# State update of a pair moved behind its prompt-state product, py in a projection bank, scaled x double buffered

## The chip, the cores and the metric

The kernel runs on one core of one Trainium2 chip. The metric is device time in microseconds (us) for one execution of the whole program. Before the change it is 2816.27 us, the median of three runs (2815.08 to 2816.45).

The engines are named as the profile names them: PE (TensorE, matmuls; PEld are its weight loads), DVE (VectorE), ACT (ScalarE), POOL (GpSimd) and SP (SyncE, which here only issues DMAs). PE writes into PSUM, which has eight banks of 128 x 512 fp32; DVE and ACT read them. "L718" is line 718 of the kernel before.

## The reference, cut to what matters

One layer for 384 tokens (256 prompt tokens, and 8 running streams of 16 tokens). The change lies in the state space branch. For each of 8 groups, with 8 heads of 64 channels and a state of 128:

```
cum = cumsum(dt * A)
y   = ((C B^T) * decay) @ (x * dt)            # within the chunk
y  += (C @ h) * exp(cum)                      # from the state that came in
h   = h * exp(last) + B^T @ (x * dt * w_end)  # the new state, an output
y  += d_skip * x;  y *= silu(z);  grouped RMSNorm
```

Before it stands the combined projection `u @ w_in` (pool, z, x/B/C, dt, gates), after it the gate products, the output projection and a squared-ReLU MLP.

## The kernel before, in words

All large products are made in three passes of 128-wide matmuls: weights and activations are split into a high and a low fp32r part, and `mm3` (L76, L77, L78) issues high x high, high x low, low x high. The weights come in tiles of 512 KB. For each tile SP issues the load (L61), ACT makes the high part `wh` (L68), DVE makes the low part `wl` by a subtraction (L69). `w`, `wh` and `wl` have three buffers each. One projection (`proj`) is two such tiles, 2 x 8 x 3 = 48 matmuls of 128 x 384 into one PSUM bank. It needs `wl` for its third matmul.

The state space stage (L496 to L856) goes through 8 groups. A group has six projections with a causal convolution behind them (B as `BT`, C as `CT`, four of x) and four of z. Behind each of them DVE reads the bank (L516 for `cbuf`, L829 for z) and the rest is DVE and ACT work on SBUF. A group's four x tiles are two pairs; a pair is `S`, its fields are:

- `hs`, the running streams' states of the pair (1 MB, loaded by `pload`, decayed by `dside` L703, updated by `state`, stored to `new_ssm_s` by a DMA that POOL issues, L731). Two buffers: a load waits until the store of the pair before last has landed.
- `trs`, the pair's x transposed, in two PSUM banks (`t_trx`); `xside` (L651) scales it twice, into `xdt` and `xdw` (four DVE operations, L656), scales `yi` into `yis` (L663), and sends the scaled x of the running streams through DRAM into another layout, `xst` (L670 to L679).
- `E`, the decay matrix times C B^T (`eside`): twelve DVE operations (L689), ACT exponentials, two DVE products (L700).
- `Y`, two banks: `t_yT` and `t_Y`. `pp`, the new prompt state: `t_pp`. `yi`, C times the incoming state: `t_yi`. `yi` of one pair and `pp` of the pair before share one bank, `py`.
- `su`, the update of the running streams' states: `state` (L710) makes four banks with eight matmuls of half height (64 rows, L718), and four DVE additions into `hs` (L727).

PSUM is two pools: two banks `mm` (`mmtile`), which projections take in turn, and six banks `ss` (`sstile`) for the rest, `py` among them.

PE's order is written out: `lump` puts a set of matmuls behind the last one issued. In a group there are two blocks of fp32 matmuls between the projections. The **first block** stands behind the fifth projection (third x): `t_cb`, `t_trB`, `t_trx` of pair 0, `t_yT` and `t_Y` of the pair before (pair 1 of the group before), `t_yi`, `t_pp`. The **second block** stands behind the tenth projection (fourth z): `t_trx` of pair 1, `t_yT`, `t_Y` of pair 0, `t_yi`, `t_pp`. `state` stands elsewhere: that of pair 0 behind the third z projection, that of pair 1 behind the CT projection of the next group. The last pair's is put into the first gate product (`gate_b(0)`, after five of its eight weight tiles), and its `Y` and `pp` follow behind that product.

On DVE, ACT, POOL and SP a scheduler sets the order when the program is built, by priority (program order) and by when it thinks operands will be there. On the chip each of these queues works in that fixed order.

`xdt` and `xdw` have one buffer each before the change, so `xside` of a pair cannot write them until `t_Y` and `t_pp` of the pair before have read them.

`gate_b` writes its three sigmoid blocks into a pool of its own, `gbp` (L484), three buffers of 128 x 512.

Of the kernel before, what the change touches and what calls it, by code (L numbers as in the profile page):

```python
# [6 lines left out]
F32 = mybir.dt.float32  # L7
# [7 lines left out]
P = 128  # L15
T = 384
TP = 256
NB = 8
# [15 lines left out]
def build(ctx, tc, io):  # L34
# [98 lines left out]
    def three(name):  # L133
        return [sstile(f"{name}_{b}") for b in range(3)]
# [346 lines left out]
            if nb == 0:  # L481
                dt_turn(srcs)

    gbp = main.enter_context(tc.tile_pool(name="gbp", bufs=3, side="right"))  # L484

    def gate_b(nb, hook=None):
        o = three(f"pj_gb{nb}")

        def done(b):
            t = gbp.tile([P, 512], F32, tag="gbt", name=f"gbt{nb}_{b}")  # L490
            s.activation(t, o[b], AF.Sigmoid, scale=yx[:, b : b + 1])
            gp.dma_start(gb_scr[nb][:, b], t)

        moving(o, [(io["w_gb"][nb, kp], f"gb{nb}_{kp}") for kp in range(8)], xg, 0, done, hook=hook)

    with tc.tile_pool(name="phd", bufs=2, reuse_waits="tile") as pd, tc.tile_pool(  # L496
# [34 lines left out]
        def lump(fn):  # L531
            with behind(last[0]):
                last[0] = fn()
# [115 lines left out]
            v.tensor_tensor(D.cbm, D.cb, cst[:, C_MASK : C_MASK + 512], ALU.mult)  # L649

        def xside(S):  # L651
            S.xdt = pd.tile([P, 2, 3, P], F32, tag="xdt", name=f"xdt{S.nm}", bufs=1)
            S.xdw = pd.tile([P, 2, 3, P], F32, tag="xdw", name=f"xdw{S.nm}", bufs=1)
            for q, tv in enumerate(S.trs):
                for o, i in ((S.xdt, 3), (S.xdw, 6)):
                    v.tensor_tensor(  # L656
                        o[:, q].rearrange("p b (h q) -> p b h q", h=2),
                        tv,
                        tok[:, i : i + 3, S.h0 + q * 2 : S.h0 + q * 2 + 2].unsqueeze(3).to_broadcast([P, 3, 2, 64]),
                        ALU.mult,  # L660
                    )
            S.yis = pd.tile([P, 2, P], F32, tag="yis", name=f"yis{S.nm}", bufs=1)
            v.tensor_tensor(  # L663
                S.yis.rearrange("p j (h q) -> p (j h) q", h=2),
                S.yi.rearrange("p (h q) -> p h q", h=4),
                tok[:, 10, S.h0 : S.h0 + 4].unsqueeze(2).to_broadcast([P, 4, 64]),
                ALU.mult,
            )
            xhl = pd.tile([P, 2, 2, P], F32R, tag="xhl", name=f"xhl{S.nm}", bufs=1)
            s.activation(xhl[:, 0], S.xdw[:, :, 2, :], AF.Copy)  # L670
            v.tensor_tensor(xhl[:, 1], S.xdw[:, :, 2, :], xhl[:, 0].bitcast(F32), ALU.subtract)
            xscr = x_scr[S.qd]
            sy.dma_start(xscr, xhl.bitcast(F32))
            S.xst = pd.tile([P, 4, 2 * P], F32R, tag="xst", name=f"xst{S.nm}", bufs=1)
            for p4 in range(4):
                for h2 in range(2):
                    sy.dma_start(
                        S.xst[h2 * 64 + p4 * 16 : h2 * 64 + p4 * 16 + 16].bitcast(F32),
                        xscr.rearrange("(q h r) l j n -> h l r q (j n)", q=4, h=2)[h2, p4 % 2],  # L679
                    )  # L680
# [26 lines left out]
                ALU.mult,  # L707
            )

        def state(S, tiles=(sstile, sstile)):  # L710
            def t_su():
                hs = S.hs.rearrange("p (r h) n -> p h r n", h=2)
                for r2, tile_ in zip((0, 2), tiles):
                    su = [tile_(f"su{S.nm}_{r2}_{h}") for h in range(2)]
                    for r in range(2):
                        for h in range(2):
                            t = slice(h * 64, h * 64 + 64)
                            i = te.matmul(  # L718
                                su[h][:, r * 256 : r * 256 + 256],
                                S.D.bs[t, r2 + r, :],  # L720
                                S.xst[t, r2 + r, :],
                                start=True,
                                stop=True,
                            )
                    for h in range(2):
                        hr = hs[:, h, r2 : r2 + 2]
                        v.tensor_tensor(hr, hr, su[h].rearrange("p (r n) -> p r n", r=2), ALU.add)  # L727
                return i

            lump(t_su)  # L730
            gp.dma_start(io["new_ssm_s"][S.qd], S.hs)  # L731
# [46 lines left out]
        for g in range(G + 1):  # L778
            if g == G:
                dside(prev.p[1])  # L780
                gate_b(0, {4: lambda: state(prev.p[1], (mmtile, sstile))})
                py = mmtile("pp_last")
                lump(lambda: t_yT(prev.p[1]))
                lump(lambda: t_Y(prev.p[1]))
                lump(lambda: t_pp(prev.p[1], py))
                final(prev.p[1])
                gate_b(1)
                finish(prev)
                break
            u0 = 17 + g * 10  # L790
            D = Pair()
            D.g = g
            D.p = [pair(D, jp) for jp in range(2)]
            D.xs, D.zs = [], []
            D.BT = conv(u0, 32 + g, "BT", 2)
            pload(D.p[0])
            if g:
                dside(prev.p[1])
            D.CT = conv(u0 + 1, 40 + g, "CT", 2)
            if g:  # L800
                state(prev.p[1])
            D.xs.append(conv(u0 + 2, g * 4, "xs", 6))
            cload(D.p[0])
            cside(D)
            D.xs.append(conv(u0 + 3, g * 4 + 1, "xs", 6))
            D.xs.append(conv(u0 + 4, g * 4 + 2, "xs", 6))
            S = D.p[0]
            lump(lambda: t_cb(D))
            mside(D)
            lump(lambda: t_trB(D))  # L810
            bside(D)
            lump(lambda: t_trx(S))
            if g:
                lump(lambda: t_yT(prev.p[1]))
                lump(lambda: t_Y(prev.p[1]))
            S.py = sstile(f"py{S.nm}")
            lump(lambda: t_yi(S))
            if g:
                lump(lambda: t_pp(prev.p[1], S.py))
            if g:  # L820
                final(prev.p[1])
            xside(S)
            D.xs.append(conv(u0 + 5, g * 4 + 3, "xs", 6))
            eside(S, 0)

            def zproj(j):
                ps = proj(in_units(u0 + 6 + j), xg, f"z{g}_{j}")
                z = pd.tile([P, T], F32, tag="zs", name=f"zs{g}_{j}", bufs=7)
                v.tensor_tensor(z, ps, rstd, ALU.mult)  # L829
                s.activation(z, z, AF.Silu)  # L830
                D.zs.append(z)

            zproj(0)
            if g:
                finish(prev)
            pload(D.p[1])
            eside(S, 1)
            zproj(1)
            dside(S)
            zproj(2)  # L840
            state(S)
            cload(D.p[1])
            zproj(3)
            S1 = D.p[1]
            lump(lambda: t_trx(S1))
            lump(lambda: t_yT(S))
            lump(lambda: t_Y(S))
            S1.py = sstile(f"py{S1.nm}")
            lump(lambda: t_yi(S1))
            lump(lambda: t_pp(S, S1.py))  # L850
            final(S)
            xside(S1)
            eside(S1, 0)
            eside(S1, 1)
            prev = D
# [20 lines left out]
    with ExitStack() as phe:  # L876
        pe1 = phe.enter_context(tc.tile_pool(name="phe", bufs=1, reuse_waits="tile"))
        pe2 = phe.enter_context(tc.tile_pool(name="phe2", bufs=3, reuse_waits="tile"))
        ab = []

        def aload():
# [7 lines left out]
                ab.append((h, l))  # L889

        for nb in (2, 3):
            gate_b(nb, {kp: aload for kp in range(8)})
        chain[0] = False
        main.close()
        mp = mpool.enter_context(tc.tile_pool(name="mp", bufs=1, side="right", reuse_waits="tile"))
        pe3 = phe.enter_context(tc.tile_pool(name="phe3", bufs=1, reuse_waits="tile"))
        for nb in range(4):
            ma = mp.tile([P, 3, 512], F32, tag="mar", name=f"mar{nb}", bufs=1)
            gb = pe3.tile([P, 3, 512], F32, tag="gbr", name=f"gbr{nb}")
            sy.dma_start(ma, ma_scr[nb])  # L900
            sy.dma_start(gb, gb_scr[nb])
            o = three(f"pj_sp{nb}")

            def done(b):
                v.tensor_tensor(gb[:, b], o[b], gb[:, b], ALU.mult)
                v.tensor_tensor(ma[:, b], ma[:, b], gb[:, b], ALU.add)

            moving(o, [(io["w_ssd"][nb, kp], f"sp{nb}_{kp}") for kp in range(16)], ab, 0, done, hook={3: merge} if nb else None)
            mtok[0] = ma
# [397 lines left out]
```

## Time and profile before

| | |
|---|---|
| median of 3 runs | 2816.27 us |
| profiled execution | 2816.05 us |
| its span, first to last instruction | 2814.3 us |
| PE busy | 2800.4 us |
| DVE busy | 1544.6 us |
| ACT busy | 1085.1 us |
| POOL busy | 88.2 us |
| PE clock granted | 0.998 |
| DMA moved | 451.39 MB |

A row of the timeline gives the start of an instruction from the start of the span, its duration, engine, line, operation, and in brackets the idle time before it and what ended it. Matmuls are pipelined, so a row's duration is longer than its step: the step is the difference of two starts. DVE operations also overlap by about 0.09 us, so for these too the step is the difference of two starts.

### The profile page before, as it was taken

Reading aid. Unit: us, or ns where it says so; the run is one execution under the profiler, and the core shown is the slowest. Engines: PE = TensorE matmul, PEld = TensorE weight load, DVE = VectorE, ACT = ScalarE, POOL = GpSimd, SP = SyncE. Lnnn points to the kernel's source line nnn. Section 1 sums busy time; section 2 is a strip of 40 time slices with the busy share of each in tenths; the row PEclk is TensorE's granted clock in tenths of the full one; section 3 lists DMA queues with packets and bytes.
Section 4 is the critical chain, followed back from the end, with each engine's and each line's share of the span. In section 5 each row is a group of like instructions: output and inputs, shape, how many; then the busy total and the mean of one; then the engine's idle time right before and its main releaser. Section 6 shows DMA issues by size and latency. Waiting matters only on the chain.

```text
span 2814.3 us, 39013 instructions
## 1 busy us (share of the span) xinstructions
PE 2800.4 (100%) x15663; PEld 2546.4 (90%) x15663; DVE 1544.6 (55%) x2219; ACT 1085.1 (39%) x1586; POOL 88.2 (3%) x143
## 2 busy tenths in 40 slices
PE   9999999999999999999999999999999999999998
PEld 8998889999999999988888888989899998989897
DVE  6575335788787878856333335434444444444446
ACT  5443224445454545434322235433233332323233
POOL 0000000010010001010000000000000000000000
PEclk9999999999999999999999999999999999999999
DMA  7434445555656566557544543433333333443433
GB/s 269 132 124 148 139 142 200 193 202 188 217 192 206 199 214 200 194 178 233 176 144 162 180 143 109 142 130 127 128 127 128 128 128 127 128 128 128 130 127 125
DMA packets 140933, 451.39 MB, mean 160 GB/s; under 512 B 17808, under 2 KB 39632, under 8 KB 135760
## 3 DMA queue, kind: packets, MB, share of 16 engines
q1 hardware_dynamic: 132624, 412.97, 44.7%
q0 software_dynamic: 8128, 35.93, 3.5%
q8 instruction: 123, 2.02, 0.3%
q14 instruction: 58, 0.48, 0.1%
HBM read 407.11 MB, written 41.72 MB: 159 GB/s over the span
## 4 chain that ended last, share of the span: by engine, by line
PE 98%; DMA 1%; DVE 0%; ACT 0%; SPq 0%; issue 0%; DVEq 0%; ACTq 0%
PE pj_up L77 6%; PE pj_up L78 6%; PE pj_up L76 6%; PE wd L108 6%; PE wd L109 6%; PE wd L107 6%; PE pj_x L76 5%; PE pj_x L78 5%; PE pj_x L77 5%; PE pj_z L76 3%; PE pj_z L78 3%; PE pj_z L77 3%; PE pj_sp L107 3%; PE pj_sp L108 3%; PE pj_sp L109 3%; PE pj_gb L107 2%
## 5 line engine op out<-in xcount | busy, mean ns | idle before, releaser
L78 PE MATMUL pj_up<-x1h,wl_up 128*128 128x384 f32 x1024 | 343.0, 335 | 0.7 <-DVE wl_up L69 0.7
L76 PE MATMUL pj_up<-x1h,wh_up 128*128 128x384 f32 x1024 | 343.2, 335 | 0.5 <-ACT x1h L1033 0.5
L77 PE MATMUL pj_up<-x1l,wh_up 128*128 128x384 f32 x1024 | 343.0, 335 | 0.6 <-DVE x1l L1038 0.6
L69 DVE TENSOR_TENSOR wl_wd<-w_wd,wh_wd 128x1024 fp32r<-128x1024 f32 x127 | 155.7, 1226 | 261.9 <-ACT wh_wd L68 261.9
L108 PE MATMUL wd<-wl_wd,hh 128*128 128x512 f32 x762 | 296.7, 389 | 0.0
L109 PE MATMUL wd<-wh_wd,hl 128*128 128x512 f32 x762 | 296.6, 389 | 0.0
L107 PE MATMUL wd<-wh_wd,hh 128*128 128x512 f32 x762 | 296.3, 389 | 0.0
L68 ACT ACTIVATE wh_wd<-w_wd 128x1024 fp32r<-128x1024 f32 x127 | 134.8, 1061 | 350.6 <-PE wd L109 284.0
L69 DVE TENSOR_TENSOR wl_up<-w_up,wh_up 128x1024 fp32r<-128x1024 f32 x128 | 156.9, 1226 | 197.7 <-ACT wh_up L68 197.5
L68 ACT ACTIVATE wh_up<-w_up 128x1024 fp32r<-128x1024 f32 x128 | 135.9, 1062 | 323.0 <-PE pj_up L77 259.8
L76 PE MATMUL pj_x<-xgh,wh_x 128*128 128x384 f32 x768 | 258.9, 337 | 0.0
L78 PE MATMUL pj_x<-xgh,wl_x 128*128 128x384 f32 x768 | 256.6, 334 | 0.0
L77 PE MATMUL pj_x<-xgl,wh_x 128*128 128x384 f32 x768 | 256.6, 334 | 0.0
L77 PEld LDWEIGHTS pj_up<-x1l,wh_up 128*128 128x128 f32 x1024 | 192.6, 188 | 1.4 <-DVE x1l L1038 1.2
L76 PEld LDWEIGHTS pj_up<-x1h,wh_up 128*128 128x128 f32 x1024 | 192.8, 188 | 1.3 <-ACT x1h L1033 1.0
L78 PEld LDWEIGHTS pj_up<-x1h,wl_up 128*128 128x128 f32 x1024 | 192.7, 188 | 1.0 <-DVE wl_up L69 1.0
L76 PE MATMUL pj_z<-xgh,wh_z 128*128 128x384 f32 x512 | 171.9, 336 | 0.0
L78 PE MATMUL pj_z<-xgh,wl_z 128*128 128x384 f32 x512 | 171.1, 334 | 0.0
L77 PE MATMUL pj_z<-xgl,wh_z 128*128 128x384 f32 x512 | 171.0, 334 | 0.0
L108 PEld LDWEIGHTS wd<-wl_wd,hh 128*128 128x128 f32 x762 | 143.0, 188 | 29.8 <-DVE wl_wd L69 0.4
L109 PEld LDWEIGHTS wd<-wh_wd,hl 128*128 128x128 f32 x762 | 143.0, 188 | 29.7
L107 PEld LDWEIGHTS wd<-wh_wd,hh 128*128 128x128 f32 x762 | 143.0, 188 | 29.6
(318 smaller groups left out, 5727.0 us busy)
## 6 DMA issues: line engine op xcount, KB each, us to landing
w_up<-w_up SPq DMA_DIRECT2D x128, 512.0 KB, 3.4
w_wd<-w_down SPq DMA_DIRECT2D x128, 512.0 KB, 3.4
w_x<-w_in SPq DMA_DIRECT2D x96, 512.0 KB, 4.8
w_z<-w_in SPq DMA_DIRECT2D x64, 512.0 KB, 3.9
w_sp<-w_ssd SPq DMA_DIRECT2D x64, 512.0 KB, 3.4
w_ga<-w_ga SPq DMA_DIRECT2D x32, 512.0 KB, 3.5
w_pp<-w_pp SPq DMA_DIRECT2D x32, 512.0 KB, 3.4
hs<-ssm SPq DMA_DIRECT2D x16, 1024.0 KB, 6.0
```

The costliest lines, as they stand in the source:

```text
L68: s.activation(h, w, AF.Copy)
L69: v.tensor_tensor(l, w, h.bitcast(F32), ALU.subtract)
L76: te.matmul(out, wh, xh, start=first, stop=False)
L77: te.matmul(out, wh, xl, start=False, stop=False)
L78: return te.matmul(out, wl, xh, start=False, stop=last)
L107: te.matmul(o[b], mh, wh[:, c], start=k == 0, stop=False)
L108: te.matmul(o[b], mh, wl[:, c], start=False, stop=False)
L109: last[0] = te.matmul(o[b], ml, wh[:, c], start=False, stop=k == nk - 1)
```

## The change

Five edits, all in the state space stage and around it:

- `state` is issued behind `t_pp`, inside the next fp32 block: pair 0's at the end of the second block, pair 1's at the end of the next group's first block, the last pair's at the end of the block between the two gate products. All its tiles come from `ss`.
- `py` comes from the `mm` pool.
- `xdt` and `xdw` take two buffers (6 KB more per partition).
- `xside` is called ahead of `state` and `final`, so that its scaling comes ahead of the sums with `Y` on DVE.
- `gate_b` takes its three blocks as one tile in a buffer of the `hs` kind (and, for the last two products, in a pool `pe4` that the later reads `gbr` share); the pool `gbp` goes.

```diff
-    gbp = main.enter_context(tc.tile_pool(name="gbp", bufs=3, side="right"))
-    def gate_b(nb, hook=None):
+    def gate_b(nb, pool, tag, hook=None):
         o = three(f"pj_gb{nb}")
+        n = NB * 256 if tag == "hs" else 1536
+        t = pool.tile([P, n], F32, tag=tag, name=f"gbt{nb}")[:, :1536].rearrange("p (b n) -> p b n", b=3)
         def done(b):
-            t = gbp.tile([P, 512], F32, tag="gbt", name=f"gbt{nb}_{b}")
-            s.activation(t, o[b], AF.Sigmoid, scale=yx[:, b : b + 1])
-            gp.dma_start(gb_scr[nb][:, b], t)
+            s.activation(t[:, b], o[b], AF.Sigmoid, scale=yx[:, b : b + 1])
+            gp.dma_start(gb_scr[nb][:, b], t[:, b])
...
-            S.xdt = pd.tile([P, 2, 3, P], F32, tag="xdt", name=f"xdt{S.nm}", bufs=1)
-            S.xdw = pd.tile([P, 2, 3, P], F32, tag="xdw", name=f"xdw{S.nm}", bufs=1)
+            S.xdt = pd.tile([P, 2, 3, P], F32, tag="xdt", name=f"xdt{S.nm}")
+            S.xdw = pd.tile([P, 2, 3, P], F32, tag="xdw", name=f"xdw{S.nm}")
...
             if g == G:
                 dside(prev.p[1])
-                gate_b(0, {4: lambda: state(prev.p[1], (mmtile, sstile))})
+                gate_b(0, pd, "hs")
                 py = mmtile("pp_last")
                 lump(lambda: t_yT(prev.p[1]))
                 lump(lambda: t_Y(prev.p[1]))
                 lump(lambda: t_pp(prev.p[1], py))
+                state(prev.p[1])
                 final(prev.p[1])
-                gate_b(1)
+                gate_b(1, pd, "hs")
...
             D.CT = conv(u0 + 1, 40 + g, "CT", 2)
-            if g:
-                state(prev.p[1])
...
-            S.py = sstile(f"py{S.nm}")
+            S.py = mmtile(f"py{S.nm}")
             lump(lambda: t_yi(S))
             if g:
                 lump(lambda: t_pp(prev.p[1], S.py))
+            xside(S)
             if g:
+                state(prev.p[1])
                 final(prev.p[1])
-            xside(S)
...
             zproj(2)
-            state(S)
             cload(D.p[1])
             zproj(3)
...
-            S1.py = sstile(f"py{S1.nm}")
+            S1.py = mmtile(f"py{S1.nm}")
             lump(lambda: t_yi(S1))
             lump(lambda: t_pp(S, S1.py))
+            xside(S1)
+            state(S)
             final(S)
-            xside(S1)
```

The scheduler's answer to it, as the two built programs show: PE's order changes only by the place of `su`. On DVE, behind the second block, one subtraction moves: the `wl` of the first half of the next group's CT projection stands ahead of the `Y` sums before, and behind the `cbuf` read of the BT projection after.

More of the change, by code (lines that the diff above doesn't have):

```diff
@@ L708, in dside, with state @@
             )
-        def state(S, tiles=(sstile, sstile)):
+        def state(S):
             def t_su():
                 hs = S.hs.rearrange("p (r h) n -> p h r n", h=2)
-                for r2, tile_ in zip((0, 2), tiles):
-                    su = [tile_(f"su{S.nm}_{r2}_{h}") for h in range(2)]
+                for r2 in (0, 2):
+                    su = [sstile(f"su{S.nm}_{r2}_{h}") for h in range(2)]
                     for r in range(2):
@@ L878, in build @@
         pe2 = phe.enter_context(tc.tile_pool(name="phe2", bufs=3, reuse_waits="tile"))
+        pe4 = phe.enter_context(tc.tile_pool(name="phe4", bufs=1, reuse_waits="tile"))
         ab = []
@@ L891, in build @@
         for nb in (2, 3):
-            gate_b(nb, {kp: aload for kp in range(8)})
+            gate_b(nb, pe4, "gbt", {kp: aload for kp in range(8)})
         chain[0] = False
@@ L895, in build @@
         mp = mpool.enter_context(tc.tile_pool(name="mp", bufs=1, side="right", reuse_waits="tile"))
-        pe3 = phe.enter_context(tc.tile_pool(name="phe3", bufs=1, reuse_waits="tile"))
         for nb in range(4):
             ma = mp.tile([P, 3, 512], F32, tag="mar", name=f"mar{nb}", bufs=1)
-            gb = pe3.tile([P, 3, 512], F32, tag="gbr", name=f"gbr{nb}")
+            gb = pe4.tile([P, 1536], F32, tag="gbt", name=f"gbr{nb}").rearrange("p (b n) -> p b n", b=3)
             sy.dma_start(ma, ma_scr[nb])
```

## The prediction, made before the changed kernel ran

> **What bounds the kernel now.** I read the page first, then PE's waits, then the timelines of PE and DVE around the two fp32 blocks of one group.
>
> ```profile
> span 2814.3 us, 39013 instructions
> ...
> PE 2800.4 (100%) x15663; PEld 2546.4 (90%) x15663; DVE 1544.6 (55%) x2219; ACT 1085.1 (39%) x1586; POOL 88.2 (3%) x143
> ...
> PE 98%; DMA 1%; DVE 0%; ACT 0%; SPq 0%; issue 0%; DVEq 0%; ACTq 0%
> ```
>
> The chain that ended last is PE for 98% of the span. So a step of PE removed is time won, and each wait of PE added is time lost. PE's waits for others (total, times, longest) hold little, for `wl` only this:
>
> ```profile
> PE pj_up L78 <- DVE wl_up L69: 0.7, 1, 0.7
> ```
>
> It is not in the state space stage, where PE does not wait at all. What the change can win there is steps between matmuls; what it can lose is new waits. The standing `su` in PE's timeline:
>
> ```profile
> 903.66 0.34 PE L78 MATMUL pj_z<-xgh,wl_z 128*128 128x384 f32 x1
> 903.93 0.75 PE L718 MATMUL su<-xst,bst 64*128 64x256 f32 x8
> 904.61 0.44 PE L76 MATMUL pj_z<-xgh,wh_z 128*128 128x384 f32 x1
> 904.88 0.34 PE L77 MATMUL pj_z<-xgl,wh_z 128*128 128x384 f32 x1
> ```
>
> and the exit of the second block into BT, the next group's first projection, with the start of CT, its second:
>
> ```profile
> 917.65 0.44 PE L76 MATMUL pj_x<-xgh,wh_x 128*128 128x384 f32 x1
> ...
> 926.08 0.33 PE L76 MATMUL pj_x<-xgh,wh_x 128*128 128x384 f32 x1
> 926.26 0.33 PE L77 MATMUL pj_x<-xgl,wh_x 128*128 128x384 f32 x1
> ```
>
> A step from one projection matmul to the next is 0.17 to 0.18 us (926.08 to 926.26); BT takes 917.65 to 926.08, 8.43 us.
>
> **What the change removes.** A projection step into `su` is 0.27 (903.66 to 903.93) and out of it 0.27 (904.61 to 904.88), each 0.10 over 0.17. `su` itself is 0.68 (903.93 to 904.61) and stays. In the block, the exit takes the place of the exit that `pp` had; the entry becomes `pp` to `su`, which no trace shows. Bounds: both extras go (0.20 per update, 3.2 us for 16) or the new entry costs twice the old (0, nothing won). I take one extra saved, 0.10 x 16 = **-1.6 us**, since the nearest row, the entry from a projection, costs 0.10. The Trainium skill (TensorEngine Tiling (Array Packing), Key Properties) says that a change of tiling mode drains the engine. `pp` (128*32) to `su` (64*128) is such a change, so by that page the entry is not free either; the rows above agree, with 0.10 us a switch.
>
> **What the change moves on DVE: the CT wait.** The trace shows DVE's instructions in the order of the program. These are its rows around the standing `su` and the second block:
>
> ```profile
> 904.51 2.47 DVE L727 TENSOR_TENSOR hs<-hs,su 128x512 f32<-128x512 f32 x4
> 906.90 1.22 DVE L69 TENSOR_TENSOR wl_x<-w_x,wh_x 128x1024 fp32r<-128x1024 f32 x1
> ...
> 913.24 0.56 DVE L829 TENSOR_TENSOR zs<-pj_z,rstd 128x384 f32<-128x384 f32 x1 [1.97 <-PE pj_z L78]
> 914.20 1.22 DVE L69 TENSOR_TENSOR wl_x<-w_x,wh_x 128x1024 fp32r<-128x1024 f32 x1 [0.40 <-ACT wh_x L68]
> 915.34 0.61 DVE L743 SCALAR_TENSOR_TENSOR xs<-xs,vec,Y 128x384 f32<-128x384 f32 x1
> ```
>
> ```profile
> 926.87 0.55 DVE L516 TENSOR_TENSOR cbuf<-pj_x,rstd 128x384 f32<-128x384 f32 x1
> 927.33 1.22 DVE L69 TENSOR_TENSOR wl_x<-w_x,wh_x 128x1024 fp32r<-128x1024 f32 x1
> ```
>
> The `wl_x` at 914.20 is the low part for CT's first half. In the changed program's order it stands behind the `cbuf` read of BT, in the place of the row at 927.33, in each of the seven groups that have a next one. CT's third matmul needs it. Between 915.34 and 926.87 DVE does not idle, so I move sums: the queue up to `cbuf` loses that `wl_x` (914.20 to 915.34, 1.14) and its wait (0.40), and gains the four additions of `su` (904.51 to 906.90, 2.39), which now come in this stretch. `cbuf` starts at 926.87 - 1.54 + 2.39 = 927.72, `wl_x` 0.46 later (926.87 to 927.33) at 928.18 and ends 1.22 on, at 929.40; a weight load puts the matmul 0.19 later, at 929.6:
>
> ```profile
> L78 PEld LDWEIGHTS pj_up<-x1h,wl_up 128*128 128x128 f32 x1024 | 192.7, 188 | 1.0 <-DVE wl_up L69 1.0
> ```
>
> PE, with `su` in the block, starts CT at 926.08 + 0.68 = 926.76 and its third matmul at 927.1. It waits 2.5 us. Even with no backlog on DVE, `cbuf` cannot be read before BT ends: about 0.2 + 0.46 + 1.22 + 0.19 - 0.35 = 1.7. I take 2.4, near the upper end because the backlog is made of rows. 7 x 2.4 = **+16.8 us**. Behind the waiting matmul stands all of PE's queue, so nothing makes it good.
>
> The last second block has the first gate product behind it, and there `wl` of the third weight tile falls behind the same backlog:
>
> ```profile
> 1205.53 0.50 PE L107 MATMUL pj_gb<-wh_gb,xgh 128*128 128x512 f32 x1
> 1205.87 0.40 PE L108 MATMUL pj_gb<-wl_gb,xgh 128*128 128x512 f32 x1
> ```
>
> ```profile
> 1214.74 2.35 DVE L69 TENSOR_TENSOR wl_gb<-w_gb,wh_gb 128x1024 fp32r<-128x1024 f32 x2
> ...
> 1226.69 2.48 DVE L727 TENSOR_TENSOR hs<-hs,su 128x512 f32<-128x512 f32 x4 [6.22 <-PE su L718]
> ```
>
> A weight tile lasts about 4.1 us there (five from 1205.53 to `su`, just ahead of 1226.69). The third tile's `wl` starts at 1214.74 - 1.54 + 2.39 = 1215.6 and serves a matmul at 1217.0; PE wants it at 1205.53 + 0.68 + 8.2 + 0.34 = 1214.8. **+2.2 us**, once.
>
> **The bank wait in the first block.** The built program gives the third and fourth `su` tile of the first block the banks of the two `trx` tiles. Their readers are the four scaled-x operations, so `su` now waits for DVE:
>
> ```profile
> 870.10 0.44 PE L76 MATMUL pj_x<-xgh,wh_x 128*128 128x384 f32 x1
> ```
>
> ```profile
> 868.25 0.61 DVE L524 SCALAR_TENSOR_TENSOR cacc<-cbuf,vec,cacc 128x384 f32<-128x384 f32 x1
> 868.77 0.61 DVE L743 SCALAR_TENSOR_TENSOR xs<-xs,vec,Y 128x384 f32<-128x384 f32 x1
> ...
> 872.22 0.55 DVE L656 TENSOR_TENSOR xdt<-trx,tok 128x384 f32<-128x384 f32 x1
> 872.68 0.55 DVE L656 TENSOR_TENSOR xdw<-trx,tok 128x384 f32<-128x384 f32 x1
> ```
>
> With two buffers the four operations come before the `Y` sums: from 868.77 on four steps of 0.47 (872.22 to 872.68) with one convolution step (0.52) among them. The last starts at 868.77 + 3 x 0.47 + 0.52 = 870.70 and ends at 871.25; with the weight load, 871.45. PE would reach the fourth tile at 870.10 + 0.34 = 870.45 to 870.5. It waits 0.95 us, in seven first blocks: **+6.7 us**. Were the scaled x where it was (872.68), it would be 3 us. In the second block the same banks are free in time: DVE's read of z starts at 913.24, four steps of 0.47 behind it end by 915.7, and `su` comes at 917.65.
>
> **The z wait.** The four additions also fall into the stretch between the first block and the third z projection:
>
> ```profile
> 894.99 0.56 DVE L141 SCALAR_TENSOR_TENSOR ny_g<-na_g,ny_g 128x384 f32<-128x384 f32 x1
> 895.58 2.21 DVE L764 SCALAR_TENSOR_TENSOR zs<-zs,vec,ny_g 128x384 f32<-128x384 f32 x4
> 897.71 0.55 DVE L829 TENSOR_TENSOR zs<-pj_z,rstd 128x384 f32<-128x384 f32 x1
> 898.17 1.22 DVE L69 TENSOR_TENSOR wl_z<-w_z,wh_z 128x1024 fp32r<-128x1024 f32 x1
> ```
>
> This `wl_z` serves the third z projection's second half, whose third matmul stands at
>
> ```profile
> 900.02 0.33 PE L78 MATMUL pj_z<-xgh,wl_z 128*128 128x384 f32 x1
> ```
>
> In the new order the z read stands ahead of the last Newton step (0.59) and the four products (2.13). It starts at 894.99 + 2.39 = 897.4; plus 0.46 + 0.59 + 2.13 + 1.22 + 0.19 the matmul could start at 902.0. PE is there at 900.02 + 0.68 + 0.95 = 901.65. Bounds 0 and 0.8 a group, 0.35 taken: 7 x 0.35 = **+2.5 us**.
>
> **What costs nothing, and its cover.** `py` in a projection bank: the projection two later waits for its readers `yis` and the copy of `pp`, a whole projection (8.4 us) away. `gate_b` in an `hs` buffer: the store of that buffer was issued a product earlier. The moved store and the load behind it:
>
> ```profile
> 907.28 0.54 POOL L731 DMA_DIRECT2D new_ssm_s<-hs  x1 [8.62 <-DVE hs L727]
> ```
>
> ```profile
> 912.33 0.33 SPq L540 DMA_DIRECT2D hs<-ssm  x1
> ...
> 928.61 4.73 SPq L61 DMA_DIRECT2D w_x<-w_in  x3
> ```
>
> The load follows the store by 5.05 us. After the change the additions end about 921, so the load is issued about 926.5, ahead of one weight load on SP's queue that before was among the three from 928.61. That tile's matmuls come after CT and half a projection, about 941; loading it takes 4.8 and splitting it 1.2 on DVE and about as much on ACT, some 7 us, so it may be issued as late as 934:
>
> ```profile
> w_x<-w_in SPq DMA_DIRECT2D x96, 512.0 KB, 4.8
> ```
>
> If that cover went, each us past it would be one of PE, in up to seven groups. POOL's other work (the sum of squares) keeps its order. `x_scr` and `xst` move forward on SP, ahead of a broadcast load that nothing needs soon.
>
> **Sum.** 16.8 + 2.2 + 6.7 + 2.5 - 1.6 = 26.6. Against the profiled execution's 2816.05 (span 2814.3 and 1.75 around it; the median of the runs is 0.2 higher): 2842.6, said as **2842 us**, 0.9% slower.
>
> **Rivals.**
> 1. Only the CT and gate waits are real, because DVE runs ahead of my sums in the first block and at z: 16.8 + 2.2 - 1.6 = 17.4, 2833 us. For it: 0.95 and 0.35 are small differences of long chains. Against: the bank reader is named in the program.
> 2. The other side, not slower: DVE has the CT `wl` ready when PE comes, and only the switch stays, 2813 to 2816 us. It decides at 927.1 minus 0.19: `wl` done by then. For it: DVE is busy 55% of the span. Against: the order puts `wl` behind a read that cannot start before BT ends, which alone costs 1.7.
> 3. The clock falls in each of the eight long waits. The start of the span shows what slow matmuls cost:
>
> ```profile
> 4.35 1.52 PE L256 MATMUL pj_p<-xgh,wh_e 128*128 128x384 f32 x3
> ...
> 6.90 0.34 PE L76 MATMUL pj_p<-xgh,wh_e 128*128 128x384 f32 x1
> ```
>
> Nine matmuls from 4.35 to 6.90 take 0.28 each, not 0.17: 1.0 us lost, and as much again if the slow phase lasts twice as long. 8 x 1 to 2 adds 8 to 16: 2850 to 2858 us. The Trainium skill (TensorE: Matmul & The Clock Gate, Part 1) puts the fall behind an idle window of about 3.4 us, more than I give any wait. No row of before has PE idle so long in mid-run.
> 4. The moved store holds SP's queue past 934, by 2 us a group: 14 more, 2856 us. It would take a store or load twice as slow as their rows.
>
> **Chances.** Forecast 78%, rival 1 9%, rival 2 5%, rival 3 4%, rival 4 4%. Bounds: low 7 x 2.0 + 1.5 + 7 x 0.4 - 3.2 = 15.1, 2831 us; high 7 x 2.6 + 2.4 + 7 x 1.3 + 7 x 0.8 = 35.3, 2851 us. This takes in rival 1 and part of rival 3. About 0.2% (5.6 us) is what a measurement of this kernel can tell from no change. Slower 95%, within 0.2% 4%, faster 1%, the last two from rival 2.
>
> **What would show it.** In PE's waits a row of CT's L78 on `wl_x` with seven times and some 2.4 us each, and one of L108 on `wl_gb`; `su` on DVE's scaled x (`xdw`), seven times, near 1 us; the entry from `pp` to `su` near 0.1 over `su`'s own step. PE's busy time is hardly changed, its idle time is up by 25. I am wrong if CT starts without a gap, or if the largest new gap is of a DMA.

## The result, and the profile after

The changed kernel takes 2857.17 us (median of 5 runs, 2856.29 to 2859.87); the kernel before, beside it, 2816.01. The ratio is 1.0149, with a 95% interval of 1.0134 to 1.0163: 41 us slower. The forecast was 2842 us, with a range of 2831 to 2851. The direction was right, the time lies outside.

The page of the changed kernel (span, busy time, chain of work that ended last):

```profile
span 2858.1 us, 39035 instructions
...
PE 2816.0 (99%) x15663; PEld 2558.1 (90%) x15663; DVE 1542.7 (54%) x2219; ACT 1101.3 (39%) x1600; POOL 94.9 (3%) x143
...
PE 84%; DVE 10%; issue 2%; DMA 2%; ACT 1%; POOL 1%; SPq 0%; DVEq 0%; POOLq 0%; ACTq 0%
```

The chain now runs through DVE for 10% of the span; before it was PE for 98%. PE's busy time is up by 15.6 us too, for the same 15663 matmuls: some of them took longer, as shown below. The profiled execution took 2859.87 us, 43.8 more than that of before, and the spans differ by the same 43.8.

PE's waits in the changed kernel (total, times, longest):

```profile
PE pj_x L78 <- DVE wl_x L69: 13.7, 7, 2.0
PE pj_z L78 <- DVE wl_z L69: 9.2, 7, 1.3
PE su L717 <- DVE xdw L655: 3.2, 7, 0.5
PE pj_gb L108 <- DVE wl_gb L69: 1.8, 2, 1.3
```

These are the places that the prediction named: CT, the third z projection, the bank in the first block, and the first gate product (1.3; the shorter wait of that row, 0.5, is in the last gate product, which it did not name). None is on a DMA.

**The CT wait, and what follows it.** PE's timeline at the start of CT in one group:

```profile
948.20 0.33 PE L76 MATMUL pj_x<-xgh,wh_x 128*128 128x384 f32 x1
948.37 0.34 PE L77 MATMUL pj_x<-xgl,wh_x 128*128 128x384 f32 x1
950.68 0.44 PE L78 MATMUL pj_x<-xgh,wl_x 128*128 128x384 f32 x1 [1.97 <-DVE wl_x L69]
...
951.42 0.52 PE L78 MATMUL pj_x<-xgh,wl_x 128*128 128x384 f32 x1
951.74 0.52 PE L76 MATMUL pj_x<-xgh,wh_x 128*128 128x384 f32 x1
...
954.60 0.34 PE L76 MATMUL pj_x<-xgh,wh_x 128*128 128x384 f32 x1
954.78 0.34 PE L77 MATMUL pj_x<-xgl,wh_x 128*128 128x384 f32 x1
```

From 948.37 to 950.68 are 2.31 us where a step is 0.17: 2.13 lost, and 0.11 more on the next step. Then, from about 951.1 to 954.6, the steps are 0.32 (951.42 to 951.74), and after that 0.18 again. This slow stretch of 3.5 us holds 11 such steps; over 0.17 each it costs 1.6 us. It follows six of the seven CT waits.

The trace records the granted clock, and it explains why one of seven goes free. In the changed kernel the clock falls to 0.50 at 544.97, 647.37, 749.77, 951.15, 1053.55 and 1155.95, for 3.41 us each time, and these starts lie 30, 60, 119, 149 and 179 times 3.413 us behind the first. So the clock changes on a grid of windows of 3.413 us. What counts is how much of a wait falls into one window. The stretches view with windows on that grid (PE's busy time first, granted clock third from the right): the fullest window of the group without a slow stretch, then two windows of the group above:

```profile
848.75:852.17 3.42, 1.92 (x11) 1.92 (x12) 3.42 (x6) 0.52 (x3) 0.00 (x0) 1.00 0.90 335
947.74:951.15 3.41, 1.45 (x9) 1.12 (x8) 3.41 (x6) 1.41 (x3) 0.00 (x0) 1.00 0.68 228
951.15:954.57 3.42, 3.42 (x12) 3.42 (x11) 3.38 (x5) 0.24 (x2) 0.00 (x0) 0.50 0.97 302
```

In the first PE is idle for 1.50 us (the other 0.45 of that wait lie in the window ahead of it) and the clock stays; in the second it is idle for 1.97 us, all of the wait, and the next window runs at half clock.

DVE at that place, in the changed kernel:

```profile
939.92 2.47 DVE L726 TENSOR_TENSOR hs<-hs,su 128x512 f32<-128x512 f32 x4
...
947.81 1.22 DVE L699 TENSOR_TENSOR E<-E,cbm 128x1024 f32<-128x1024 f32 x1
948.94 0.55 DVE L515 TENSOR_TENSOR cbuf<-pj_x,rstd 128x384 f32<-128x384 f32 x1
949.41 1.21 DVE L69 TENSOR_TENSOR wl_x<-w_x,wh_x 128x1024 fp32r<-128x1024 f32 x1
```

The low part of CT's first tile (949.41) stands behind BT's `cbuf` read, and that behind all of the block's work, without a gap.

**The blocks.** PE at the end of a first block, then of the second one behind it:

```profile
888.10 1.09 PE L612 MATMUL py<-Bk,xdw 128*32 128x128 f32 x32
889.12 0.84 PE L717 MATMUL su<-xst,bst 64*128 64x256 f32 x6
890.42 0.47 PE L717 MATMUL su<-xst,bst 64*128 64x256 f32 x2 [0.46 <-DVE xdw L655]
890.81 0.45 PE L76 MATMUL pj_x<-xgh,wh_x 128*128 128x384 f32 x1
...
938.07 1.09 PE L612 MATMUL py<-Bk,xdw 128*32 128x128 f32 x32
939.10 0.74 PE L717 MATMUL su<-xst,bst 64*128 64x256 f32 x8
939.77 0.45 PE L76 MATMUL pj_x<-xgh,wh_x 128*128 128x384 f32 x1
940.05 0.34 PE L77 MATMUL pj_x<-xgl,wh_x 128*128 128x384 f32 x1
```

In the first, `su` takes 1.69 (889.12 to 890.81): 1.02 over its time in the second, of which the row shows 0.46 as a wait for the fourth scaled x. In the second, `pp` takes 1.03 (938.07 to 939.10), `su` 0.67, and the first step of the projection 0.28.

**The z wait.** PE's rows, then DVE's ahead of it:

```profile
920.57 0.34 PE L77 MATMUL pj_z<-xgl,wh_z 128*128 128x384 f32 x1
922.23 0.45 PE L78 MATMUL pj_z<-xgh,wl_z 128*128 128x384 f32 x1 [1.33 <-DVE wl_z L69]
922.52 0.34 PE L76 MATMUL pj_z<-xgh,wh_z 128*128 128x384 f32 x1
```

```profile
901.04 0.56 DVE L148 TENSOR_TENSOR nl_g<-ssum,nh_g 128x384 fp32r<-128x384 f32 x1 [1.00 <-ACT nh_g L147]
902.12 0.42 DVE L521 TENSOR_SCALAR cacc<-cbuf,vec 128x384 f32<-128x384 f32 x1 [0.52 <-ACT cbuf L517]
...
917.78 0.55 DVE L828 TENSOR_TENSOR zs<-pj_z,rstd 128x384 f32<-128x384 f32 x1
```

PE's step is 1.66 (920.57 to 922.23), 1.49 over 0.17, and the next one 0.29: 1.60 lost. DVE idles 1.00 and 0.52 us on the group norm (`nh_g` waits for the sum of squares) and on a copy of ACT behind it, and is late for z afterwards.

**The balance of a group**, from one second block to the next: 95.96 us before, 102.0 after in six groups and 100.4 in the one without the slow stretch. 2.24 (CT) + 1.60 (slow stretch) + 1.60 (z) + 1.02 (first block) - 0.40 (two updates, below) = 6.06. Over the seven groups it is 40.8 us. The first second block starts 1.2 us earlier than before, mostly because pair 0's `su` now stands inside it. From the last second block on 4.2 are lost: 0.7 is that `su`, about 1.5 the first gate product (1.29 of it as a wait), and 2.1 the last gate product, in many small waits for low parts; no run here isolates the cause of these 2.1.

### The profile page after: what moved, and what is told of

The parts are those of the page before. It is cut to its first block, busy times and chain, and to the rows that moved or that the text cites. A ratio compares the mean times of both kernels' runs of the same rounds, so it can differ in the third digit from the quotient of the medians.

```text
span 2858.1 us, 39035 instructions
## 1 busy us (share of the span) xinstructions
PE 2816.0 (99%) x15663; PEld 2558.1 (90%) x15663; DVE 1542.7 (54%) x2219; ACT 1101.3 (39%) x1600; POOL 94.9 (3%) x143
## 4 chain that ended last, share of the span: by engine, by line
PE 84%; DVE 10%; issue 2%; DMA 2%; ACT 1%; POOL 1%; SPq 0%; DVEq 0%; POOLq 0%; ACTq 0%
PE pj_up L78 6%; PE pj_up L77 6%; PE pj_up L76 6%; PE wd L109 6%; PE wd L108 6%; PE wd L107 6%; PE pj_x L78 4%; PE pj_x L76 4%; PE pj_x L77 3%; PE pj_sp L108 3%; PE pj_sp L107 3%; PE pj_sp L109 3%; PE pj_p L76 2%; PE pj_ga L107 2%; PE pj_ga L108 2%
```

## The experiments

The ratio is against the kernel before, run on the same chip (medians of 2814.5 to 2815.3 us).

| run | us | ratio, 95% interval |
|---|---|---|
| e1_state_back | 2836.35 | 1.0076 [1.0061, 1.0091] |
| e2_ct_early | 2833.65 | 1.0067 [1.0052, 1.0082] |
| e3_second_only | 2843.73 | 1.0103 [1.0088, 1.0118] |
| e4_sums_then_su | 2840.32 | 1.0089 [1.0072, 1.0106] |
| e5_single_buffer | 2814.89 | 0.9999 [0.9990, 1.0008] |
| e6_double_ct_first | 2814.49 | 0.9997 [0.9988, 1.0007] |
| e7_all_mended | 2813.02 | 0.9992 [0.9983, 1.0001] |
| e8_longer_wait | 2869.28 | one run |
| e9_su_single | 2855.72 | 1.0151 [1.0134, 1.0167] |
| e10_ct_and_sums | 2822.89 | 1.0029 [1.0018, 1.0039] |

### e1: the state back where it was

Against the changed kernel:

```diff
             D.CT = conv(u0 + 1, 40 + g, "CT", 2)
+            if g:
+                state(prev.p[1])
...
-            xside(S)
             if g:
-                state(prev.p[1])
                 final(prev.p[1])
+            xside(S)
...
             zproj(2)
+            state(S)
...
-            xside(S1)
-            state(S)
             final(S)
+            xside(S1)
```

and the last pair's in the first gate product, as before.

> The changed kernel with the state updates and the order of scaled x and sums where they were before; what stays of the change is py in a projection bank, two buffers of scaled x, and the gate products' buffer. My theory (the loss is made by the order on DVE and by su's bank in the first block, none by the banks and buffers): 2816 to 2818 us, no PE wait in the state space stage, granted clock 1.00 throughout. Rival (py in a projection bank makes a projection wait for its readers, or the second pair of buffers costs something): a part of the 41 us stays, 2822 us or more, with a PE wait on ACT or DVE in a bank pj_x.

My theory fell: half of the loss is still there, and `su` is not in a block at all. PE's waits in e1:

```profile
PE pj_x L78 <- DVE wl_x L69: 9.0, 14, 0.7
PE pj_gb L108 <- DVE wl_gb L69: 3.4, 2, 2.6
PE pj_x L76 <- ACT wh_x L68: 2.6, 7, 0.4
```

A group is 98.4 to 98.5 us, 2.5 over before. Behind the wait of 2.6 us in the first gate product the clock falls too, once. DVE in e1, at the end of the second block:

```profile
934.66 1.22 DVE L699 TENSOR_TENSOR E<-E,cbm 128x1024 f32<-128x1024 f32 x1
935.80 2.35 DVE L69 TENSOR_TENSOR wl_x<-w_x,wh_x 128x1024 fp32r<-128x1024 f32 x2
938.07 0.55 DVE L515 TENSOR_TENSOR cbuf<-pj_x,rstd 128x384 f32<-128x384 f32 x1
```

CT's low part (the first of the two `wl_x` at 935.80) stands behind `E` here, though still ahead of BT's `cbuf` read, where in the kernel before it stands ahead of the first sum with `Y` (the row at 914.20 in the prediction), right behind the read of the fourth z. New theory: with one buffer, scaled x can't be made until the block's `Y` and `pp` have been read, so that when the order is set DVE has nothing to do behind the z read, and the low part of the next projection but one goes there. With two buffers, scaled x is ready at once; the block's work has priority, and the low part goes behind all of it. e5, e6 and e9 test this.

### e5: of the change, only the bank of py and the gate's buffer

```diff
-            S.xdt = pd.tile([P, 2, 3, P], F32, tag="xdt", name=f"xdt{S.nm}")
-            S.xdw = pd.tile([P, 2, 3, P], F32, tag="xdw", name=f"xdw{S.nm}")
+            S.xdt = pd.tile([P, 2, 3, P], F32, tag="xdt", name=f"xdt{S.nm}", bufs=1)
+            S.xdw = pd.tile([P, 2, 3, P], F32, tag="xdw", name=f"xdw{S.nm}", bufs=1)
```

on top of e1.

> As e1_state_back, but scaled x with one buffer again: of the change only py in a projection bank and the gate products' buffer are left. Theory (new, after e1): the second buffer of scaled x alone made e1's 21 us, since scaled x no longer waits for the block's end, so that the scheduler finds no gap on DVE for the low part of CT's first tile and puts it behind all of the block's work, E included. Then this is the kernel before again: ratio 0.999 to 1.001. Rival (py in a projection bank, or the gate buffer, costs part of it): ratio 1.003 or more, with PE waits on ACT or DVE in the state space stage.

0.9999, and no wait of PE in the stage; a group is 95.96. So `py` in a projection bank and the gate's buffer cost nothing, as predicted, and the second buffer of scaled x, by itself and with `su` left where it was, costs 0.76% (e1).

### e6: two buffers, with CT's low part put first

On top of e1. The weights of BT and of CT's first half are split ahead of the block, and the block's sums and scaled x are issued behind CT's low part on DVE; so are the bank reads of the projections behind it. In the last group the first gate product's first three weight tiles take the place of BT and CT:

```diff
             zproj(3)
+            if g < G - 1:
+                ahead(in_units(u0 + 10), f"x{33 + g}", (0, 1))
+                ahead(in_units(u0 + 11), f"x{41 + g}", (0,))
+            else:
+                ahead([io["w_gb"][0, kp] for kp in range(3)], "gb0", range(3))
+            wct = lw[0]
...
-            final(S)
-            xside(S1)
-            eside(S1, 0)
+            with behind(wct):
+                final(S)
+                xside(S1)
+                eside(S1, 0)
```

`ahead` makes the high and low parts early, `lw[0]` is the last low part, `behind` the edge that PE's order is written with.

> As e1_state_back (two buffers of scaled x, state where it was), but the low part of CT's first tile is put on DVE ahead of the second block's sums and scaled x, and those of the projections behind it ahead of the bank reads. Theory: the second buffer costs only by displacing that low part and the load behind it on SP; ratio 0.999 to 1.001, no wait on wl_x. Rival (the second buffer costs something else, such as scaled x's own transfers ahead of the weight loads): e1's waits on wh_x and the second wl_x stay, 7 x 1.3 us: ratio 1.003 to 1.004.

0.9997, a group 95.96, no wait of PE in the stage. The second buffer costs only by what it displaces.

### e2: the changed kernel, with CT's low part put first

The same edges but that of the gate, in the changed kernel (`state(S)`, `final(S)` and `eside(S1, 0)` behind `wct`, `xside(S1)` free).

> The changed kernel with the low part of CT's first weight tile forced on DVE ahead of the second block's sums and additions (and that of the third and fourth projections ahead of the bank reads before them). My theory: the CT wait (2.24 a group, seven times) and the half-speed phase behind it (1.6 us, six times) go together, 15.7 + 9.6 = 25.3 us: 2832 us, clock 1.00 in every 40 us window. Rival 1 (the clock falls for another cause than the wait, such as the fp32 block being longer): only 15.7 go, 2841.5 us, and the 0.96 windows stay. Rival 2 (the wait only moves to the next tile, since the queue is as long as before): 2850 us or more, PE waits on wl_x in another projection.

DVE in e2, the fourth z read and the low part that now follows it after one scaled x:

```profile
921.65 0.56 DVE L842 TENSOR_TENSOR zs<-pj_z,rstd 128x384 f32<-128x384 f32 x1 [1.97 <-PE pj_z L80]
...
922.61 1.23 DVE L69 TENSOR_TENSOR wl_x<-w_x,wh_x 128x1024 fp32r<-128x1024 f32 x1
```

No CT wait, no slow stretch in any group, and from `t_trx` of the second block to that of the next first block 48.21 us where the changed kernel has 52.0 and the kernel before 48.40. CT's wait and the slow stretch behind it go together; the rival that had them apart (2841.5) is out. The z wait is still there, in two groups at 1.7 instead of 1.3.

### e3: only pair 0's state in a block

Pair 1's back behind CT, pair 0's in the second block as changed.

> Only pair 0's state is in an fp32 block (the second one); pair 1's stands behind CT as before. My theory: CT wait 7 x 2.24 and six half-speed phases of 1.6 stay, the first block's bank wait (1.02) and the z wait (1.60) go, 0.20 a group is won: 2816 + 15.7 + 9.6 + 1.8 (gate) - 1.6 = 2841.5 us. Rival (the z wait comes of the scaled x being ahead of the sums, not of the additions in the first block): the z wait stays, about 2850 us.

The z wait falls to 0.2, so it needs su's additions in the first block. CT's wait is 1.95 in each group as expected, but the slow stretch follows it in three of seven, not six; and there is a wait of 0.70 on a low part in the projection behind CT that I had not seen. The two about balance: 2843.7 for 2841.5.

### e4: the sums with Y ahead of su's additions

```diff
             xside(S)
             if g:
-                state(prev.p[1])
                 final(prev.p[1])
+                state(prev.p[1])
```

and the same in the second block.

> The changed kernel with the sums with Y (final) ahead of su's four additions on DVE in both blocks; su stays in the blocks, scaled x stays first. My theory: the z wait is 1.60 because the sum of squares starts after su's additions, so that DVE idles 1.5 us on the group norm; with the sums first, these 1.5 us go and the z wait falls to 0.1 to 0.4: about 9 us less, 2848 us; CT wait and first-block wait stay. Rival (the z wait is the four additions' 2.4 us of DVE time alone, wherever they stand): unchanged, 2857 us.

DVE in e4, the three rows that answer to those of the z wait above:

```profile
890.83 0.55 DVE L148 TENSOR_TENSOR nl_g<-ssum,nh_g 128x384 fp32r<-128x384 f32 x1
891.40 0.42 DVE L521 TENSOR_SCALAR cacc<-cbuf,vec 128x384 f32<-128x384 f32 x1
...
907.34 0.56 DVE L828 TENSOR_TENSOR zs<-pj_z,rstd 128x384 f32<-128x384 f32 x1 [0.19 <-PE pj_z L78]
```

The two idle stretches are gone, the z read now waits for PE and not PE for it, and from `t_trx` of the first block to that of the second are 48.65 us, 1.35 less than in the changed kernel (50.0): the z wait falls from 1.60 to 0.25, as expected. The time is 8 us below what I expected, and that is the clock: CT's wait is 1.97 in all seven groups as before, but the slow stretch follows only one of them. Five times 1.6 is 8. In the trace a group is 99.1 us, close to 29 windows of 3.413 us (99.0), so the wait keeps nearly the same place in the grid from group to group: between 1.39 and 1.86 us of it fall into one window, and the clock falls behind the 1.86 alone.

### e10: both mends

e2 and e4 together; the bank wait of the first block is left in.

> The changed kernel with both single mends, that of e2_ct_early (CT's low part first) and that of e4_sums_then_su (sums ahead of su's additions); the third x convolution's taps stay where they are, so su's bank in the first block stays late. Theory (the losses add up): left are the first block's wait, 1.02 a group, the rest of the z wait, 0.25, and the gate's 1.8, less 3.2 for the switches: 8.9 + 1.8 - 3.2 = 7.5 us, ratio 1.0027, half speed nowhere. Rival (with no CT wait PE reaches z earlier against DVE, and the z wait comes back): z wait 1.3 to 1.6, ratio 1.0055 to 1.0065.

1.0029 for 1.0027. The waits of `su` (7 times 0.46) and of the gate are the only ones left in the stage. So the losses add up, and what the bank wait costs is seen by itself.

### e7: all of them

e10, and: the third x convolution's taps (four DVE operations) behind the first block's scaled x; the low part of the next z ahead of each z read and of the Newton steps; the norm's four products behind the third z projection; the gate's first low parts ahead of the last two blocks' sums and additions.

```diff
-            D.xs.append(conv(u0 + 4, g * 4 + 2, "xs", 6))
+            rest = conv(u0 + 4, g * 4 + 2, "xs", 6, split=True)
...
             xside(S)
             if g:
                 final(prev.p[1])
                 state(prev.p[1])
+            D.xs.append(rest())
```

> The changed kernel (su in both blocks, two buffers of scaled x) with DVE's order mended at each place where PE waited: low parts of the next tiles ahead of the bank reads and of the block's sums and additions (CT, z, gate); the sums with Y ahead of su's additions; the third x convolution's taps behind the first block's scaled x, so that su's third bank is free in time; the norm's products behind the third z projection. Theory: no PE wait in the stage is left and only the two saved switches remain, 0.20 us an update, 3.2 us for 16: ratio 0.9985 to 0.9995. Rival (DVE has no room for su's additions at these places and a wait comes back somewhere): ratio 1.002 or more. Rival 2 (the saved switch is an artefact of the rows and gives no time): ratio 1.000.

PE in e7 at the end of the first block (L83 is the first matmul of `mm3` here):

```profile
866.46 1.09 PE L630 MATMUL py<-Bk,xdw 128*32 128x128 f32 x32
867.48 0.74 PE L735 MATMUL su<-xst,bst 64*128 64x256 f32 x8
868.15 0.45 PE L83 MATMUL pj_x<-xgh,wh_x 128*128 128x384 f32 x1
```

`pp` takes 1.02 and `su` 0.67, without the 1.02 us that the changed kernel loses here. No wait of PE is left in the stage, and each of the seven groups is 95.55 us, 0.41 below before: 0.20 for each update. That is what the change can give, 3.2 us for 16 updates. The time agrees with it (median 1.9 us below before) but its interval still holds 1.

### e8: a longer wait, for the clock

In the changed kernel, extra DVE operations ahead of the low part of CT's first tile (their results are not used):

```diff
+            for _ in range(0 if g == 0 else (1 if g < 5 else 2)):
+                extra[0] = v.tensor_tensor(seg(dm), cbuf[(ncv[0] - 1) % 3][:, :, 3:], seg(rstd), ALU.mult)
             D.CT = conv(u0 + 1, 40 + g, "CT", 2)
```

> The changed kernel with extra DVE operations of 128 x 384 (results unused) between BT's cbuf read and the low part of CT's first tile: one in the first four groups, two in the last three (convolution steps come between them). CT's wait becomes some 2.8 and 3.7 us. Theory: the half-speed phase is one fixed stretch of about 3.5 us that follows when enough of such a stretch was idle, by chance with 2 us (10 of 21 so far), more often with 2.8, always with 3.7: at least 6 of the 7 groups show it, each with 11 or so steps at 0.32 us, and 1.6 us lost whatever the wait's length. Rival 1 (the loss grows with the wait): 2.3 and 3 us of loss, 15 or more slow steps. Rival 2 (chance alone, half of the groups whatever the length): 3 or 4 of 7.

PE in e8, in two groups with the same wait (L81 is the third matmul of `mm3` here):

```profile
545.21 0.44 PE L81 MATMUL pj_x<-xgh,wl_x 128*128 128x384 f32 x1 [2.90 <-DVE wl_x L70]
...
749.29 0.69 PE L81 MATMUL pj_x<-xgh,wl_x 128*128 128x384 f32 x1 [2.90 <-DVE wl_x L70]
749.77 0.52 PE L79 MATMUL pj_x<-xgh,wh_x 128*128 128x384 f32 x1
750.09 0.52 PE L80 MATMUL pj_x<-xgl,wh_x 128*128 128x384 f32 x1
...
755.47 0.33 PE L79 MATMUL pj_x<-xgh,wh_x 128*128 128x384 f32 x1
```

Behind 545.21 the steps are 0.17 at once (not shown); behind 749.29 they are 0.32 for 18 steps, 5.8 us. Of the four waits of 2.9 us three have a slow stretch, of the three of 3.9 all. That part of the theory held (six of seven). The fixed length seen in the matmuls did not: the stretches have 8 to 18 slow steps (2.6 to 5.8 us), one begins 0.9 us after the wait, and they cost 1.3 to 2.8 us (group against group, an extra us allowed for the longer wait), with no order by its length. The record of the clock shows the order. Each fall starts on the grid and lasts one window (3.41 us, three times) or two (6.83, three times), and it can start while PE still waits, so that fewer slow matmuls are seen. It lasted two where PE was still idle for 0.74, 1.51 and 1.84 us of the first slow window, and one where that was 0.57 or less. The wait at 545.21 is cut by a window's border into 1.44 and 1.46, and the clock stays.

### e9: su in both blocks, with one buffer

```diff
-            xside(S1)
-            state(S)
             final(S)
+            xside(S1)
+            state(S)
```

in both blocks, with the two buffers of scaled x taken back to one, as in e5.

> su in both blocks, but scaled x with one buffer, so behind the sums with Y as before the change. Theory (it is the second buffer that displaces CT's low part, since scaled x then need not wait for the block): DVE is free while the block runs and takes that low part there, so no CT wait, though su's additions stand in the same block. What it costs instead: su's last banks wait for scaled x, which now waits for pp: about 2.9 us in the first block and 1.0 in the second; and in the built order another low part (two projections on) stands behind a cbuf read, some 3 us; with the saved 0.4 and a part of the half-speed phases 7 to 9.5 us a group: 2865 to 2882 us. Rival (the prediction's reason: su's additions by themselves put CT's low part behind BT's cbuf read): a CT wait of 2 us or more, seven times.

There is no CT wait: the low part is back behind the fourth z read, with su's additions in the same block. So the rival, which is the prediction's reason, is out. (e9 also puts the sums ahead of su's additions; e4 does that with two buffers, and CT's wait stays.) What I expected in its place was wrong: su waits only 0.2 in the first block and not at all in the second. The loss is in the fourth projection behind the second block, on ACT:

```profile
PE pj_x L76 <- ACT wh_x L68: 14.0, 7, 2.0
PE pj_x L78 <- DVE wl_x L69: 8.0, 7, 1.2
```

```profile
965.05 0.24 ACT L517 COPY cbuf<-cbuf 128x45 f32<-128x45 f32 x1 [4.27 <-DVE cbuf L515]
...
965.32 2.00 ACT L68 ACTIVATE wh_x<-w_x 128x1024 fp32r<-128x1024 f32 x2
```

ACT idles 4.27 us on a copy that needs the end of one projection, with the next projection's high part behind it. It is the same fault on another queue. PE waits 2.0 us there and 1.2 more on the low part 1.8 us later, and the slow stretch stands behind the two in five of seven groups.

## Why the prediction was right and where it was wrong

- **The CT wait** (2.4 predicted): 2.24 measured, in the predicted place, seven times. Its place in the queue was read rightly from the built order, but the reason given for its length named only su's additions. It takes two causes. The second buffer of scaled x, which the prediction took as free, moves the low part behind the block's work: alone it costs 0.76% (e1 against e5). With su's additions in the block too, the low part falls behind BT's `cbuf` read and the wait grows from 0.6 (e1) to 2.0 (the changed kernel, e3). Additions without the second buffer give no CT wait (e9).
- **The slow stretch** was rival 3, with a chance of 4%, and here the prediction failed first: its sum put the slow clock at nothing, and it took 6 x 1.6 = 9.6 us. It came behind waits of 2 us. The Trainium skill (TensorE: Matmul & The Clock Gate, Part 1) ties half rate to an idle window of some 3.4 us that runs freely, whatever the kernel does. The trace agrees with the window: in every run the falls in the state space stage lie on a grid of 3.413 us, and the grid's place against the start of the span differs from run to run. It does not agree that the window must be idle throughout. Of all windows of that grid in this stage and the first gate product, in all runs, the clock fell behind each of the 19 with 1.91 us of idle PE or more, behind none of those (at full clock) with 1.84 or less, and behind three of five between. The 21 waits of 1.91 to 1.98 us in the changed kernel, e3 and e4 divide by this into 10 with a fall and 11 without; the 26 waits of 1.27 to 1.73 us in these runs, e2 and e8 are too short for it.
- **What before showed of it.** The prediction let the page's figure hold down the chance of this rival, though the trace of before could have contradicted it, at the start of the MLP (the stretches view again, windows on that run's grid):

```profile
1740.01:1743.43 3.42, 1.90 (x11) 1.25 (x10) 2.75 (x8) 1.57 (x6) 0.00 (x0) 1.00 0.00 0
1743.43:1746.84 3.41, 3.41 (x12) 3.41 (x11) 3.09 (x8) 2.29 (x7) 0.00 (x0) 0.50 0.00 0
```

PE is idle for 1.52 us of the first window, in three waits of 0.9 us at most, at transposes and the first matmuls behind them, and the clock falls in the second. Rival 3's own time, 2850 to 2858 us, holds the measured 2857, but by luck: the slow clock is 9.6 of the difference, and most of the rest is the next item.

- **The z wait** was mis-sized: 0.35 predicted, 1.60 measured, 8.8 us over seven groups. The term moved the queue by the additions' 2.39 us but left the idle time of DVE out: with the sums with `Y` behind the additions, the sum of squares is late, and DVE idles 1.5 us (e4 takes this away, and 0.25 is left of the wait).
- **The first block** (0.95): 1.02, with the bank and the fourth scaled x that the prediction named.
- **The gate** (2.2): about 1.5 in the first gate product, 1.29 of it as a wait. The 2.1 in the last gate product had no term in the sum.
- **The saved switches** (1.6): 3.2. `pp` takes 1.03 into `su` and in the kernel before 1.02 into a projection, so the entry costs 0.01 and both extras go, the upper bound. The Trainium skill (TensorEngine Tiling (Array Packing), Key Properties) has a drain at each change of tiling mode; between 128*32 and 64*128 this trace shows none above 0.01, between a projection and `su` 0.10.
- Rival 4 did not happen: the moved load and store of the states land in 4.9 us each and no PE wait is on a DMA.
- Of the signs given, the waits came where they were said to come. PE's idle time is up by 28 us (25 said), but its busy time by 15.6, where "hardly changed" was said; 9.6 of this is the slow clock; the rest is lost at the same places as the waits, in steps that the profile counts as busy.

The profiled execution (2859.87) lies 17.2 us over the sum's 2842.6: 9.6 of slow clock, 8.8 at z, 1.4 at the gate and 0.5 in the first block, less 1.6 for the switches and 1.1 for CT, make 17.6. The median lies lower by 2.7; only the profiled execution has a trace.

What stays open: where the grid of windows lies in an execution, which nothing in these runs sets, and so how many slow stretches it will have; why 1.52 us of idle PE are enough at the start of the MLP and not in the state space stage; and the 2.1 us in the last gate product.

## What to carry to other kernels

A buffer more can make a queue worse: it makes work ready earlier, and where the order goes by priority that work takes the gap in which a low-priority operation with an early due time used to run. Look for what now stands in that gap, on every queue (DVE in e1, ACT in e9), before you price the gain. A wait of the matmul engine of 2 us or more is to be priced with the clock behind it: here 1.6 us when some 1.9 us of it fell into one window of the clock's grid, which for waits of 2 us was 10 times in 21; and in a moved sum, the idle time that its consumers bring belongs to the price.

## What the hardware did that I had not expected

The granted clock changes on a grid of 3.413 us, and in this stage 1.91 us of idle PE within one window were enough for a window at half speed, where 1.84 were not; two equal waits differ only in how the grid cuts them. And a switch between two kinds of small tiles (`pp` to `su`) costs 0.01 us, where one between a projection and `su` costs 0.10 each way.
